# Row maxima of a 64 MB array: loads issued alternately from the SP and the Activation queue

## The chip, the cores and the metric

One core of one Trainium2 chip. The metric is the device time of one execution in microseconds (us); the median of several executions is quoted. More than one chip took part, so each kernel is compared with the runs of the kernel before made in the same series.

## The reference

```python
def setup_inputs():
    batch, seq, dim = 32, 512, 1024
    return {"x": np.random.randn(batch, seq, dim).astype(np.float32)}

def reference(x):
    return np.max(x, axis=-1).astype(np.float32)
```

That is 16,384 rows of 1,024 floats: 64 MB are read, 64 KB written.

## The kernel before

Each of the 128 partitions owns 128 consecutive rows. 112 of them come as 28 "bulk" tiles of four rows (2 MB each), the last 16 as 8 "tail" tiles of two rows (1 MB). Every tile is loaded by one DMA and reduced by one instruction on the vector engine (DVE) into a column block of `res`. There are two stores, one after the bulk and one at the end.

```python
    GB = 4
    GT = 2
    TAIL_ROWS = 16
    NB = (I - TAIL_ROWS) // GB      # 28
    NT = TAIL_ROWS // GT            # 8
    SPLIT = I - TAIL_ROWS           # 112

    bulk = ctx.enter_context(tc.tile_pool(name="bulk", bufs=10))
    tailp = ctx.enter_context(tc.tile_pool(name="tailp", bufs=5))
    # ... (res, out_r, xr)
    for c in range(NB):
        b = c * GB
        xc = bulk.tile([P, GB, D], mybir.dt.float32)
        nc.sync.dma_start(out=xc, in_=xr[:, b:b + GB, :])
        nc.vector.reduce_max(out=res[:, b:b + GB], in_=xc, axis=mybir.AxisListType.X)

    nc.scalar.dma_start(out=out_r[:, :SPLIT], in_=res[:, :SPLIT])

    for t in range(NT):
        b = SPLIT + t * GT
        xt = tailp.tile([P, GT, D], mybir.dt.float32)
        nc.sync.dma_start(out=xt, in_=xr[:, b:b + GT, :])
        nc.vector.reduce_max(out=res[:, b:b + GT], in_=xt, axis=mybir.AxisListType.X)

    nc.scalar.dma_start(out=out_r[:, SPLIT:], in_=res[:, SPLIT:])
```

The framework under it adds the semaphores; two things of it show in the traces. It keeps at most eight DMAs in flight, counted over both queues, and it may move a store past a load on its queue.

## Time and profile before

| | before |
|---|---|
| time, median of 4 runs | 166.98 us (166.93 to 167.51) |
| span of the profiled execution | 166.5 us |
| DMA engines | full, some 428 GB/s from 4 to 158 us |
| DVE | 85% busy; 4.42 us a bulk tile, which lands every 4.89 us |
| last bulk reduce starts / last reduce ends | 141.82 / 164.09 us |

How to read the lines in the prediction: in the slices each digit is the busy tenths of one fortieth of the span. A group has its source line, engine, operation, output and input, then the count, busy time and mean duration in ns, and after the second bar the idle time just before, with what ended it. In a timeline the first two numbers are start and duration in us, `x7` is seven instructions merged into one row, and the bracket holds the idle time before and its cause. `SPq` and `ACTq` are issues on the two queues. A ring is the list of transfers that one queue has pending on one DMA engine; a packet is one record of such an engine, here one row of a tile (16 KB in the bulk, 8 KB in the tail).

### The profile page before, as it was taken

To read this page: it belongs to the slowest core of one execution; us is meant where nothing else is said; L and a number is where in the kernel's file an instruction comes from. 1 tells how busy PE (TensorE), PEld (TensorE's weight loads), DVE (VectorE), ACT (ScalarE), POOL (GpSimd) and SP (SyncE) were. 2 spreads that over 40 slices of the span, in tenths; PEclk is the share of its full clock that TensorE was granted. 3 is DMA by queue.
4 is the path that set the end of the run, shared out by engine and by line. 5 is a ranking of instruction groups with operands and counts; after the bars stand their busy time and mean duration, and the time that the engine had idled before them with its cause. 6 is when DMAs were issued, how large, how long until landed. Compare 5 with 4: busy or idle time off the path is not lost.

```text
span 166.5 us, 142 instructions
## 1 busy us (share of the span) xinstructions
DVE 141.4 (85%) x36; POOL 0.2 (0%) x4
## 2 busy tenths in 40 slices
DVE  0098887898888798888898888899888889999994
POOL 0000000000000000000000000000000000000000
DMA  5999999999999999999999999999999999999950
GB/s 189 429 441 429 429 394 425 433 437 429 433 421 354 425 433 429 429 429 429 433 421 429 429 429 437 417 429 433 429 433 421 425 433 411 425 417 423 421 222 2
DMA packets 5472, 67.18 MB, mean 404 GB/s; under 512 B 864, under 2 KB 864, under 8 KB 864
## 3 DMA queue, kind: packets, MB, share of 16 engines
q1 hardware_dynamic: 5184, 67.11, 95.7%
q10 hardware_dynamic: 288, 0.07, 0.2%
HBM read 67.11 MB, written 0.07 MB: 403 GB/s over the span
## 4 chain that ended last, share of the span: by engine, by line
DMA 89%; DVE 8%; SPq 1%; issue 0%
DMA xc<-in_x_dram 84%; DMA xt<-in_x_dram 5%; DVE res L59 5%; DVE res L47 3%; SPq L46 1%
## 5 line engine op out<-in xcount | busy, mean ns | idle before, releaser
L47 DVE TENSOR_REDUCE res<-xc 128x4 f32<-128x4096 f32 x28 | 123.8, 4420 | 22.5 <-DMA xc<-in_x_dram 22.5
L59 DVE TENSOR_REDUCE res<-xt 128x2 f32<-128x2048 f32 x8 | 17.8, 2280 | 0.2 <-DMA xt<-in_x_dram 0.2
L80 POOL MEMSET const-bfloat16-1.0<- 128x1 bf16 x1 | 0.1, 103 | 0.0
L80 POOL MEMSET const-uint8-127<- 128x1 uint8 x1 | 0.1, 103 | 0.0
L80 POOL MEMSET const-float32-1.0<- 128x1 f32 x1 | 0.1, 100 | 0.0
L80 POOL MEMSET const-float32-0.0<- 128x1 f32 x1 | 0.1, 99 | 0.2 <-issue 0.2
## 6 DMA issues: line engine op xcount, KB each, us to landing
xc<-in_x_dram SPq DMA_DIRECT2D x28, 2048.0 KB, 39.1
xt<-in_x_dram SPq DMA_DIRECT2D x8, 1024.0 KB, 23.5
out_dram<-res ACTq DMA_DIRECT2D x1, 56.0 KB, 6.8
out_dram<-res ACTq DMA_DIRECT2D x1, 8.0 KB, 1.4
```

What stands on the lines that cost most here:

```text
L46: nc.sync.dma_start(out=xc, in_=xr[:, b:b + GB, :])
L47: nc.vector.reduce_max(out=res[:, b:b + GB], in_=xc, axis=mybir.AxisListType.X,)
L59: nc.vector.reduce_max(out=res[:, b:b + GT], in_=xt, axis=mybir.AxisListType.X,)
L80: nc = _bacc.Bacc("TRN2", target_bir_lowering=False, num_devices=1)
```

## The change

Loads go in turn to the SP queue (`nc.sync`) and the Activation (ACT) queue (`nc.scalar`), with the intent that no single queue's issuing holds up the transfers.

```diff
     for c in range(NB):
         b = c * GB
         xc = bulk.tile([P, GB, D], mybir.dt.float32)
-        nc.sync.dma_start(out=xc, in_=xr[:, b:b + GB, :])
+        (nc.sync, nc.scalar)[c % 2].dma_start(out=xc, in_=xr[:, b:b + GB, :])
 ...
     for t in range(NT):
         b = SPLIT + t * GT
         xt = tailp.tile([P, GT, D], mybir.dt.float32)
-        nc.sync.dma_start(out=xt, in_=xr[:, b:b + GT, :])
+        (nc.sync, nc.scalar)[t % 2].dma_start(out=xt, in_=xr[:, b:b + GT, :])
```

## The prediction

> **What bounds the kernel now.** I read the page of the kernel before from the top, and first the slices of the span with the DMA totals.
>
> ```profile
> span 166.5 us, 142 instructions
> DVE 141.4 (85%) x36; POOL 0.2 (0%) x4
> DVE  0098887898888798888898888899888889999994
> DMA  5999999999999999999999999999999999999950
> GB/s 189 429 441 429 429 394 425 433 437 429 433 421 354 425 433 429 429 429 429 433 421 429 429 429 437 417 429 433 429 433 421 425 433 411 425 417 423 421 222 2
> ```
>
> The 16 DMA engines are full from the second slice to the thirty-eighth, at about 428 GB/s. VectorE (DVE) is nearly as busy, 85%, which matters below. Next the groups and the waits: which engine waits for which.
>
> ```profile
> L47 DVE TENSOR_REDUCE res<-xc 128x4 f32<-128x4096 f32 x28 | 123.8, 4420 | 22.5 <-DMA xc<-in_x_dram 22.5
> L59 DVE TENSOR_REDUCE res<-xt 128x2 f32<-128x2048 f32 x8 | 17.8, 2280 | 0.2 <-DMA xt<-in_x_dram 0.2
> ...
> SPq L46 <- DMA xc<-in_x_dram: 90.5, 20, 5.4
> ```
>
> The first line: every bulk reduce waits for its load, 8.24 us for the first and 0.47 for most others. The last line, from the waits of the SP queue: the queue stands waiting 90.5 us, and 20 of the 28 bulk issues wait for a load to land. 28 less 20 is 8: eight loads are in flight, and the ninth is issued at 8.23 us, when the first lands. So issuing is not short of anything: the queue is eight loads (39 us from issue to landing) ahead. Last the timeline of the end.
>
> ```profile
> 136.92 4.42 DVE L47 TENSOR_REDUCE res<-xc 128x4 f32<-128x4096 f32 x1 [0.47 <-DMA xc<-in_x_dram]
> 141.82 4.42 DVE L47 TENSOR_REDUCE res<-xc 128x4 f32<-128x4096 f32 x1 [0.48 <-DMA xc<-in_x_dram]
> 146.16 15.47 DVE L59 TENSOR_REDUCE res<-xt 128x2 f32<-128x2048 f32 x7
> 146.27 0.38 ACTq L53 DMA_DIRECT2D out_dram<-res  x1
> 148.47 4.71 SPq L58 DMA_DIRECT2D xt<-in_x_dram  x3
> 161.80 2.29 DVE L59 TENSOR_REDUCE res<-xt 128x2 f32<-128x2048 f32 x1 [0.17 <-DMA xt<-in_x_dram]
> 164.12 0.34 ACTq L65 DMA_DIRECT2D out_dram<-res  x1
> ```
>
> Loads land every 4.89 us (136.92 to 141.82), a reduce takes 4.42. From 141.82 on, DVE runs without a gap: the last bulk reduce and seven tail reduces (2.19 us from start to start) fill the 19.8 us in which the tail's 8 MB arrives, and the last tail reduce waits just 0.17 us for its load. Both limits meet there: DMA has priority by 0.17 us. Any bulk tile that comes later than today at the end makes DVE the bound.
>
> **What the Trainium skill says.** "DMA: Bandwidth & Descriptors", section "Issuing engines are not separate DMA queues": DMAs from SP, ACT and GpSimd run on the same 16 engines, and a second issuer saves only sequencer time. The trace agrees in what it can show: the engines are full with one issuer, and the sequencer's time, 0.33 us an issue against 4.89 us of transfer, is hidden.
>
> The same page, section "Queues, rings and completion order": SP and ACT own one ring each on every engine, and an engine takes turns between rings that have work, packet by packet. The packet records of before show it at one place: the 56 KB store from the ACT queue has 8 rows on each engine, and while tail loads run, these rows come one every 0.327 us, that is one 8 KB load packet (0.31) and one store row (0.025) in turn. The store takes so 6.8 us to land, against 1.4 for the 8 KB store of equally many rows at the end.
>
> "Perfetto Trace Analysis", section "DMA Instruction — HWDGE (DVE, Sync)": the descriptor generator is locked by one instruction at a time. Before can't show two issuers at the start; if so, ACT's first load gets its descriptors some 0.37 us (the first issue's duration) after SP's.
>
> **The change part by part.** It removes no instruction and no byte. 14 bulk and 4 tail issues move to the ACT queue.
>
> 1. Issue time: 18 × 0.33 = 6 us leave SP. All lay beside transfers. Gain: 0; at the very start at most 0.3 us, as engines draw their first packet at 1.74 us and the second queue can't move that.
> 2. Bytes: 64 MB at 428 GB/s is 157 us, as now. A bulk row of 16 KB takes 0.611 us on its engine and 8 of them 4.89, exactly the spacing of landings: there is no bubble between loads that a second ring could fill. Gain: 0.
> 3. Order of landing: this is the cost. Today load c has all engines to itself. With two rings in turn, loads c and c+1 share them, each takes 9.78 us, and if both rings start together they land together. DVE starts at about 13.0 instead of 8.24, which costs nothing itself (it has 0.47 us spare per load). What counts is the end. Call L the number of 16 KB packets by which SP's ring leads ACT's on each engine; strict turns keep L as it is. The last bulk data lands at about T = 141.8 as today, plus L × 0.31 (the 8 KB tail packets that SP's ring has then already moved); load 26, on SP's ring, lands at T − L × 0.611. From the start of load 26's reduce with both loads there, DVE needs 2 × 4.34 (start to start, 141.82 to 146.16) + 7 × 2.19 + 2.29 = 26.3 us without a gap; today it needs 22.27 from 141.82 to 164.09.
>    - L = 0: load 26 at 141.8, DVE ends at 168.1: +4.0 us.
>    - L = 1 (SP merely first in each turn): 141.2, end 167.5: +3.4.
>    - L = 4 (rings half a load apart): loads land evenly again, load 26 at 139.4, 27 at 143.0; reduce 27 starts at 143.7, DVE ends at 165.7: +1.6.
>    - L = 8 (SP a whole load ahead): loads 25 and 26 land together at 136.9, 27 at 144.3; reduce 27 starts after two others, at 145.6; end 167.6: +3.5.
> 4. The tail's own waits: tail loads 5 to 7 need buffers of tails 0 to 2 and are issued some 3 us later than today (148.47, 150.66, 152.85). They then land at about 157 to 162, and DVE, late itself, wants the last at 163 to 166. Hidden.
> 5. What follows the last reduce (2.4 us to the span's end) stays, and the time is 0.5 above the span, as before.
>
> **Where L falls.** Both queues leave the starting barrier at the same time. The generator's lock puts ACT about 0.4 us behind, which alone is L = 1. But the store on ACT shows that an engine has more already taken in: its first row moved 3.5 us after its issue began, against 1.0 for the first load of the run, so some 2.5 us of SP's packets stood ahead. If that happens at the start, L is about 4. I give L of 0 or 1 about 0.35, 2 to 6 about 0.45, 7 or 8 about 0.2: mean +2.8 us.
>
> **The rivals.**
> - Nothing happens or a small gain: two rings hide a bubble or the slow spots (slices with 394 and 354 GB/s). Against it: packets follow each other at 0.611 us and the slow spots are packets of 1.2 to 2.4 us on half of the engines, not missing descriptors. It would give 165.5 to 167.
> - The store as a block: the first store now stands in ACT's in-order queue with four tail loads and waits for the last bulk reduce. If tail loads 1 and 3 stand behind it, they are issued only at about 150, land at 155 or later, and DVE waits some 3 us more: 173 to 174. Against it: in before, the tail issues are at 107.55, 112.44 and 122.24, and none at the landing of 117.3, so the store took that place in the order of semaphores; it is moved past tail loads rather than kept where the code has it. I give it 0.06.
> - Two streams of rows disturb each other in HBM and the rate falls: 1% is 1.6 us more, 171 to 172. The trace speaks neither for nor against it, as SP's loads had no second load beside them.
> - Paired landing with L from 0 to 8, as worked out: 168.6 to 171.0.
>
> **Range and chances.** 166.98 + 2.8 = 169.8; a little weight on the first rival takes it to 169.7. Low 168.0 (even staggering, faster start), high 171.8 (pairs and 0.5% less rate). The 2% line is 170.3, or +3.34 us: reached with L of 0, 1 or 8, a blocked tail or a lower rate. That makes slower 0.33, within 2% 0.64, faster 0.03.
>
> **What would show it.** The DMA slices should read about 428 GB/s as before, the loads' time to landing stay near 39 us, and the first reduce start between 10.5 and 13 us instead of 8.24. Right: DVE's waits of bulk reduces come in pairs, one long and one near zero (or even, if L is near 4), and DVE runs from load 26 to the end without a gap, with load 26's landing and the DVE end matching one line of the list. Wrong, if a bulk load lands 4.89 us after its predecessor from 8.24 on (no taking turns), if the last tail reduce still waits for its load, if the slices show another rate, or if a tail reduce waits for a load on ACT that was issued after the first store.

## The result

The changed kernel took 171.2 us (median of 4 runs, 171.16 to 171.23) against 166.98: ratio 1.0243, 95% interval 1.0228 to 1.0258, so it is slower by 2.4%. (A ratio here and below is the mean time of one kernel's fast runs over that of the other's of the same rounds, so not quite the ratio of the medians.) The page of the changed kernel, for slices, totals and groups:

```profile
span 169.4 us, 142 instructions
DVE 140.0 (83%) x36; POOL 0.2 (0%) x4
DVE  0008979798997979799797979979797997999994
DMA  5999999999999999999999999999999999999900
GB/s 174 433 422 433 433 433 433 426 433 433 433 422 433 426 418 426 430 426 433 426 433 433 433 430 426 433 422 418 430 422 433 433 420 418 422 383 344 373 29 2
...
L47 DVE TENSOR_REDUCE res<-xc 128x4 f32<-128x4096 f32 x28 | 122.4, 4414 | 27.0 <-DMA xc<-in_x_dram 27.0
L59 DVE TENSOR_REDUCE res<-xt 128x2 f32<-128x2048 f32 x8 | 17.6, 2276 | 0.0
...
xc<-in_x_dram ACTq DMA_DIRECT2D x14, 2048.0 KB, 39.1
xc<-in_x_dram SPq DMA_DIRECT2D x14, 2048.0 KB, 39.1
```

The DMA engines run at the old rate for the old length and a load still lands 39.1 us after its issue. What is new is at both ends. DVE starts a slice later. At the end DVE is full (9) in both kernels, but the transfers now fall behind it: 383, 344, 373 and 29 GB/s in slices 36 to 39, against 417, 423, 421 and 222 before. The tail reduces wait for nothing, 0.0, where the last one before waited 0.17 us for its load. The timeline of the changed kernel, its beginning and its end:

```profile
0.73 0.39 ACTq L46 DMA_DIRECT2D xc<-in_x_dram  x1
0.73 0.37 SPq L46 DMA_DIRECT2D xc<-in_x_dram  x1
...
13.38 8.74 DVE L47 TENSOR_REDUCE res<-xc 128x4 f32<-128x4096 f32 x2 [13.38 <-DMA xc<-in_x_dram]
23.17 8.74 DVE L47 TENSOR_REDUCE res<-xc 128x4 f32<-128x4096 f32 x2 [1.04 <-DMA xc<-in_x_dram]
...
140.69 8.74 DVE L47 TENSOR_REDUCE res<-xc 128x4 f32<-128x4096 f32 x2 [1.06 <-DMA xc<-in_x_dram]
149.35 17.63 DVE L59 TENSOR_REDUCE res<-xt 128x2 f32<-128x2048 f32 x8
149.47 0.35 ACTq L53 DMA_DIRECT2D out_dram<-res  x1
151.66 4.72 ACTq L58 DMA_DIRECT2D xt<-in_x_dram  x2
167.01 0.35 ACTq L65 DMA_DIRECT2D out_dram<-res  x1
```

Reduces now come in twos: 9.79 us from pair to pair, one wait of 1.04 us for two tiles. The semaphore records show why: loads 0 and 1 landed at 13.36 and 13.53, loads 26 and 27 at 140.66 and 140.84. So at 140.69 DVE has two bulk tiles in hand, where before it had one at 141.82, and from there it works without a gap: 8.66 for two bulk tiles, 17.63 for the tail, ending at 166.98. Before, it ended at 164.09.

### The profile page after: what moved, and what is told of

It reads as the page before. It is cut to its first block, busy times and chain, and to the rows that moved or that the text cites. A ratio compares the mean times of both kernels' runs of the same rounds, so it can differ in the third digit from the quotient of the medians.

```text
span 169.4 us, 142 instructions
## 1 busy us (share of the span) xinstructions
DVE 140.0 (83%) x36; POOL 0.2 (0%) x4
## 4 chain that ended last, share of the span: by engine, by line
DMA 82%; DVE 14%; DVEq 1%; SPq 0%; issue 0%
DMA xc<-in_x_dram 82%; DVE res L59 9%; DVE res L47 5%; DVEq L91 1%; SPq L46 0%
## 5 line engine op out<-in xcount | busy, mean ns | idle before, releaser
L47 DVE TENSOR_REDUCE res<-xc 128x4 f32<-128x4096 f32 x28 | 122.4, 4414 | 27.0 <-DMA xc<-in_x_dram 27.0
## 6 DMA issues: line engine op xcount, KB each, us to landing
xc<-in_x_dram ACTq DMA_DIRECT2D x14, 2048.0 KB, 39.1
xc<-in_x_dram SPq DMA_DIRECT2D x14, 2048.0 KB, 39.1
```

## The experiments

My theory: an engine takes the two rings in turn, so partner loads land together, and DVE, which has no slack at the end, gets its last bulk tiles in a lump. Rivals: the ACT queue is a slower issuer; two rings lower the transfer rate; the tail loads are held behind the store in the ACT queue; or the cost lies outside the span, since the two profiles differ by 2.9 us and the times by 4.2. Twelve kernels ran, in three series of four.

**1. The kernel before again.** No edit.

> The unchanged kernel as its own control. Every theory expects a ratio of 1.000 within 0.3%, 167.0 us. It is also a second look at two points of the first profile: the two slow spots of the loads (at 23 and 51 us, together some 1.2 us) and the gap between span and time, which was 0.5 us there and is 1.8 us for the changed kernel. If the slow spots belong to that one execution, this profile shows the last bulk load landing at about 140.4 instead of 141.8 and a span of about 165.2, 1.8 us below the time; if they belong to the kernel, the span is 166.5 again and the missing 1.3 us of the changed kernel lie outside its span.

Measured 167.66 us, ratio 0.9978 (0.994 to 1.0017). Its four executions and the seven beside it all have a time 1.73 to 1.86 us above their span, as have the four of the changed kernel. So none of the loss lies outside the span. The spans of the four quoted executions of before are not on record. If the same 1.8 us holds for them, the profile with 166.5 us belongs to an execution of about 168.3 us, longer than the four; a typical one has a span of 166.98 - 1.8 = 165.2, and the change cost 4.2 us in spans as in times. What can make executions of before differ is in the packet records: at 23 us, and again at 51, eight of the sixteen DMA engines had a packet of 1.2 to 2.4 us instead of 0.611. Here they were at 23, 38 and 75 us. The expectation left two cases open, and it was a mix: the slow spots come each time, at changing places and sizes.

**2. The mirror: all loads on ACT, the stores on SP.**

```diff
-        nc.sync.dma_start(out=xc, in_=xr[:, b:b + GB, :])
+        nc.scalar.dma_start(out=xc, in_=xr[:, b:b + GB, :])
-    nc.scalar.dma_start(out=out_r[:, :SPLIT], in_=res[:, :SPLIT])
+    nc.sync.dma_start(out=out_r[:, :SPLIT], in_=res[:, :SPLIT])
```
(and likewise for the tail and the last store)

> All loads from the Activation queue, both stores from SP: still one ring for the loads. Theory (partners of two rings land together and the vector engine has no slack at the end): nothing lands together, so 167.0 us, ratio 1.000 within 0.5%. Rival (loads issued from Activation are themselves slower or start later): at least half of the change's loss, 169 us or more.

Measured 167.64 us, ratio 0.9983 (0.9947 to 1.0019). The ACT queue is as good an issuer as SP; that rival falls.

**3. Two queues, one tile.** Each tile's halves on the two queues:

```diff
-        nc.sync.dma_start(out=xc, in_=xr[:, b:b + GB, :])
+        H = GB // 2
+        nc.sync.dma_start(out=xc[:, :H, :], in_=xr[:, b:b + H, :])
+        nc.scalar.dma_start(out=xc[:, H:, :], in_=xr[:, b + H:b + GB, :])
```
(the tail likewise, a row each)

> Both queues, but the two halves of one tile: rows 0 and 1 of each bulk tile from SP, rows 2 and 3 from Activation, and one row each in the tail. Packets take turns as in the changed kernel, but partners now serve the same reduce. Theory: tiles are complete every 4.89 us as before, first reduce at about 8.5, 167.0 us within 0.7. Rival (two rings in turn lower the rate of the DMA engines, or cost something outside the span): 170 us or more, with the slices below 428 GB/s or the gap of time over span larger than in the control.

Measured 170.61 us, ratio 1.0156 (1.0116 to 1.0196): my number was missed and the rival's was met. The timeline of the split kernel:

```profile
8.62 4.42 DVE L49 TENSOR_REDUCE res<-xc 128x4 f32<-128x4096 f32 x1 [8.62 <-DMA xc<-in_x_dram]
13.59 4.42 DVE L49 TENSOR_REDUCE res<-xc 128x4 f32<-128x4096 f32 x1 [0.55 <-DMA xc<-in_x_dram]
```

Tiles are indeed complete one by one again, from 8.62 us, but every 4.97 us. Halving the tile had changed a second thing, the length of a row: 8 KB packets took 0.311 us, not half of 0.611. Experiment 5 takes this apart.

**4. Stagger: hold back the first ACT load.** (against the changed kernel)

```diff
         xc = bulk.tile([P, GB, D], mybir.dt.float32)
+        if c == 1:
+            nc.gpsimd.memset(xc[:, 0, :1024], 0.0)
         (nc.sync, nc.scalar)[c % 2].dma_start(out=xc, in_=xr[:, b:b + GB, :])
```

> The changed kernel, with the first Activation load held back by a memset of 1024 columns of its tile on GpSimd, some 1 to 3 us. Theory: SP's ring then leads by L packets of 16 KB, L being the hold in us over 0.611, and keeps that lead to the end; partners land apart by the 0.2 us of the changed kernel plus twice the hold (both measured late in the run, up to 4.9 us), load 26 lands earlier by one hold, and the time falls below 171.2 by about the hold, for a hold of 2.4 us to 168.7. Rival (the loss is in the DMA rate, in the issue or outside the span): time unchanged at 171.2 or longer by the hold, as loads start later.

Measured 169.03 us, ratio 1.0055 (1.0017 to 1.0094) against 1.0243 of the change. The timeline of the staggered kernel:

```profile
0.73 0.95 POOL L47 MEMSET xc<- 128x1024 f32 x1 [0.29 <-POOLq L82]
...
1.71 103.38 ACTq L48 DMA_DIRECT2D xc<-in_x_dram  x14
...
134.07 13.07 DVE L49 TENSOR_REDUCE res<-xc 128x4 f32<-128x4096 f32 x3 [1.04 <-DMA xc<-in_x_dram]
147.06 17.63 DVE L61 TENSOR_REDUCE res<-xt 128x2 f32<-128x2048 f32 x8
```

Starting loads later made the kernel faster by 2.3 us (span 167.1 against 169.4, last reduce ending at 164.69 against 166.98). A loss of rate, or of time to issue, would not shrink when loads start later. The hold was 0.98 us (the 1 to 3 us expected were a guess that no run stood behind), and a gain of about the hold was expected; the lead was more: SP's loads landed at 10.72, 20.50, 30.29 and ACT's at 16.59, 26.37, that is 5.87 and 3.91 us apart in turn. ACT's first packet moved at 5.50, SP's at 1.73. A hold of 1 us let 2 us more of SP's packets go ahead. The lead of 5.87/2 = 2.9 us is 4.8 packets by the landings, and it was kept through the bulk (loads 24 and 25 at 128.19 and 134.05). Loads 26 and 27, at 137.98 and 142.05, are closer, as SP's ring had by then gone over to the shorter rows of the tail.

**5. The control of experiment 3: both halves from SP.**

```diff
-        nc.scalar.dma_start(out=xc[:, H:, :], in_=xr[:, b + H:b + GB, :])
+        nc.sync.dma_start(out=xc[:, H:, :], in_=xr[:, b + H:b + GB, :])
```
(against experiment 3; the tail likewise)

> The control for the split tile: the same two halves of each tile, but both from SP. The split kernel came out at a ratio of 1.0156 and its tiles were complete every 4.97 us instead of 4.89. If that comes from the smaller packets (8 KB rows took 0.311 us, 16 of them 4.98), this kernel has the same 4.97 with one queue and a ratio of 1.011 to 1.022. If it comes from two rings taking turns, tiles come every 4.89 us here and the ratio is within 0.5% of 1.

Measured 169.69 us, ratio 1.0085 (1.0027 to 1.0142), a little under the range. The timeline:

```profile
8.40 4.42 DVE L49 TENSOR_REDUCE res<-xc 128x4 f32<-128x4096 f32 x1 [8.40 <-DMA xc<-in_x_dram]
13.37 4.42 DVE L49 TENSOR_REDUCE res<-xc 128x4 f32<-128x4096 f32 x1 [0.55 <-DMA xc<-in_x_dram]
```

With one queue tiles come every 4.97 us too. The small rows, not the second ring, cost 27 × 0.08 = 2.2 us of the bulk. Experiments 3 and 5 differ by 0.9 us in the medians of two series; that rest is not settled. Experiment 3's profile has 1.3 us of waits in its tail, this one 0.6.

**6. Only the bulk alternates.**

```diff
-        (nc.sync, nc.scalar)[t % 2].dma_start(out=xt, in_=xr[:, b:b + GT, :])
+        nc.sync.dma_start(out=xt, in_=xr[:, b:b + GT, :])
```
(against the changed kernel)

> Only the bulk loads alternate, the tail is all on SP. Theory: the vector engine is late by the last bulk pair and runs without a gap from there, so the tail's queue doesn't matter: ratio 1.021 to 1.027 as for the whole change. Rival (the loss comes from tail loads behind the store in the Activation queue, or from tail loads landing in pairs): less than half of the loss, ratio below 1.012.

Measured 171.47 us, ratio 1.0183 (1.0128 to 1.0239): below the range, and by the ratio alone unclear, as its interval takes in the 2% line; this series' runs of before were scattered (167.31 to 169.49). But the time is that of the whole change (171.2, in another series) and the span, 169.5, too. The end of its timeline:

```profile
140.81 8.75 DVE L47 TENSOR_REDUCE res<-xc 128x4 f32<-128x4096 f32 x2 [1.03 <-DMA xc<-in_x_dram]
149.47 17.62 DVE L59 TENSOR_REDUCE res<-xt 128x2 f32<-128x2048 f32 x8
149.59 0.35 ACTq L53 DMA_DIRECT2D out_dram<-res  x1
```

No tail load is on ACT, so the store can hold none back, and the loss is there in full. That rival falls.

**7. Only the tail alternates.**

```diff
-        (nc.sync, nc.scalar)[c % 2].dma_start(out=xc, in_=xr[:, b:b + GB, :])
+        nc.sync.dma_start(out=xc, in_=xr[:, b:b + GB, :])
```
(against the changed kernel)

> Only the eight tail loads alternate. Theory: bulk loads land evenly as before; only tail partners share engines, and if the last two land together the last reduce starts 2.2 us after the last landing, so +1 to +2 us, ratio 1.006 to 1.012, with waits of the tail reduces for their loads. Rival as in the run before this: most of the loss is here, ratio above 1.015. It has one ring in the bulk, so if the slow spots (half of the engines with packets of 1 to 2 us, seen in each one-queue profile and in no two-queue one) belong to one ring, they are here again, and not in the run with the bulk alternating.

Measured 172.31 us, ratio 1.024 (1.0172 to 1.0308): about twice the +1 to +2 us that I expected, and by the ratio as much as the whole change (1.0243), though this interval takes in the 2% line too. Bulk loads do not come in pairs here, and the store did not do it: the tail reduces wait for nothing. Its timeline:

```profile
111.84 12.60 ACTq L58 DMA_DIRECT2D xt<-in_x_dram  x2
...
117.35 4.42 DVE L47 TENSOR_REDUCE res<-xc 128x4 f32<-128x4096 f32 x1 [1.09 <-DMA xc<-in_x_dram]
124.10 4.42 DVE L47 TENSOR_REDUCE res<-xc 128x4 f32<-128x4096 f32 x1 [2.34 <-DMA xc<-in_x_dram]
129.62 4.42 DVE L47 TENSOR_REDUCE res<-xc 128x4 f32<-128x4096 f32 x1 [1.10 <-DMA xc<-in_x_dram]
136.38 4.42 DVE L47 TENSOR_REDUCE res<-xc 128x4 f32<-128x4096 f32 x1 [2.34 <-DMA xc<-in_x_dram]
```

Two tail loads were issued on ACT at 111.84 and 124.1, into a ring with nothing in it. They took every other turn from the bulk loads queued on SP and landed at 123.17 and 135.40, before bulk loads 23 (124.08) and 25 (136.35), though DVE needed them only after load 27. The bulk was late by their bytes: load 27 landed at 146.15, against 141.37 in experiment 1, and DVE ended at 168.13 against 163.66. It is the theory's principle in a form that I had not foreseen: two rings give up the order of arrival. In the full change ACT's tail loads stand behind ACT's own bulk loads and can't overtake.

**8. A longer tail.** The changed kernel with `TAIL_ROWS = 32`.

> The changed kernel with the last 32 instead of 16 rows as two-row tiles. Theory: the last four-row pair lands at 121.1 and 121.3 (as measured), so the vector engine starts its run without a gap there and needs 2 x 4.34 + 15 x 2.19 + 2.29 us: 164.9, and with the last pair landing together at about 161.1 not before 165.6, against 167.0 in the changed kernel: ratio about 1.013 (1.008 to 1.018). Rival (the loss doesn't depend on the slack of the vector engine): ratio 1.024 or, with more and smaller transfers, above.

Measured 170.58 us, ratio 1.013 (1.0073 to 1.0188). The end of its timeline:

```profile
121.28 8.75 DVE L47 TENSOR_REDUCE res<-xc 128x4 f32<-128x4096 f32 x2 [1.06 <-DMA xc<-in_x_dram]
129.94 26.64 DVE L59 TENSOR_REDUCE res<-xt 128x2 f32<-128x2048 f32 x12
...
156.78 2.29 DVE L59 TENSOR_REDUCE res<-xt 128x2 f32<-128x2048 f32 x1 [0.20 <-DMA xt<-in_x_dram]
```

Given more small tiles DVE caught up: from 156.78 on it waits for loads again. About half of the loss is gone, as expected.

**9 and 10. Half the work for DVE** (results wrong, each reduce reading 512 of its 1,024 columns), on the kernel before and on the changed one.

```diff
-            in_=xc,
+            in_=xc[:, :, :D // 2],
```
(and `xt` likewise)

> Wrong result on purpose: the kernel before, each reduce reading only the first 512 of its 1024 columns, so the vector engine's work is about halved (2.3 us for a bulk tile as for 2048 elements in the tail, 1.2 in the tail) and the loads are unchanged. The last reduce waits for the last load: 1.1 us less than the kernel before, ratio 0.990 to 0.997.

> Wrong result on purpose: the changed kernel with halved reduces, pair to the run before this. Theory (the loss is the vector engine's missing slack behind partners that land together): only the last tail pair still costs, one reduce of 1.1 us, less what the one-ring loads lose in their slow spots: ratio to the kernel before 0.990 to 1.001, at most 1 us above its half-work partner, where the change itself cost 4 us. Rival (the loss is in the transfers, the issue or the store): 3 us or more above its partner, ratio 1.012 or more.

Measured 166.67 us (ratio 0.9928, 0.9879 to 0.9977) and 166.53 us (0.9912, 0.9869 to 0.9954), beside 167.84 of the kernel before: both within what was expected. With slack on DVE the alternation costs nothing. The last lines of the two timelines, half-work before and then half-work changed:

```profile
158.84 1.22 DVE L59 TENSOR_REDUCE res<-xt 128x2 f32<-128x1024 f32 x1 [1.27 <-DMA xt<-in_x_dram]
161.30 1.22 DVE L59 TENSOR_REDUCE res<-xt 128x2 f32<-128x1024 f32 x1 [1.24 <-DMA xt<-in_x_dram]
```

```profile
150.77 2.34 DVE L59 TENSOR_REDUCE res<-xt 128x2 f32<-128x1024 f32 x2 [2.63 <-DMA xt<-in_x_dram]
153.42 1.22 DVE L59 TENSOR_REDUCE res<-xt 128x2 f32<-128x1024 f32 x1 [0.30 <-DMA xt<-in_x_dram]
158.52 3.50 DVE L59 TENSOR_REDUCE res<-xt 128x2 f32<-128x1024 f32 x3 [3.88 <-DMA xt<-in_x_dram]
```

Tiles still land in lumps in the second (three reduces in a row at 158.52), and DVE now swallows them.

**11. Alternate in the first 16 bulk loads only.**

```diff
-        nc.sync.dma_start(out=xc, in_=xr[:, b:b + GB, :])
+        (nc.scalar if c % 2 and c < 16 else nc.sync).dma_start(out=xc, in_=xr[:, b:b + GB, :])
```

> The change in the first 16 bulk loads only (8 from Activation, 8 from SP); the other 12 bulk loads and the tail all from SP. Theory: the pair of loads 14 and 15 leaves the vector engine 4 us late; with loads again every 4.89 us and reduces every 4.34 it makes up 0.55 a load and is level by about load 23, so nothing is left at the end: ratio 0.993 to 1.003, and the last tail reduce waits for its load or starts with it. Rival (alternating costs in proportion to the loads it touches): 16 of 36, ratio about 1.010.

Measured 167.48 us (6 runs), ratio 0.9965 (0.9931 to 0.9999). The end of its timeline:

```profile
140.94 4.42 DVE L47 TENSOR_REDUCE res<-xc 128x4 f32<-128x4096 f32 x1 [0.47 <-DMA xc<-in_x_dram]
145.28 15.48 DVE L59 TENSOR_REDUCE res<-xt 128x2 f32<-128x2048 f32 x7
160.92 2.29 DVE L59 TENSOR_REDUCE res<-xt 128x2 f32<-128x2048 f32 x1 [0.17 <-DMA xt<-in_x_dram]
```

Sixteen alternating loads cost nothing at the end: DVE was level again from load 23 (its reduce at 121.37 waited for its load), and the last lines are those of the kernel before.

**12. A try at a faster version:** experiment 11 with `TAIL_ROWS = 24`, and the last two-row tile loaded and reduced row by row.

```diff
-        nc.sync.dma_start(out=xt, in_=xr[:, b:b + GT, :])
-        nc.vector.reduce_max(out=res[:, b:b + GT], in_=xt, axis=mybir.AxisListType.X)
+        step = GT if t < NT - 1 else 1
+        for r in range(0, GT, step):
+            nc.sync.dma_start(out=xt[:, r:r + step, :], in_=xr[:, b + r:b + r + step, :])
+            nc.vector.reduce_max(out=res[:, b + r:b + r + step], in_=xt[:, r:r + step, :],
+                                 axis=mybir.AxisListType.X)
```

> A try at a version faster than both: as the run before this, with 24 rows in two-row tiles at the end instead of 16, and the last of them loaded and reduced as two single rows. The longer tail lets the vector engine be level with the loads before the end (it gains 0.3 us per two-row tile), and then the last reduce is of one row, 1.15 us instead of 2.29; some 0.2 us are lost to smaller rows. Ratio 0.989 to 0.997. If the vector engine isn't level by then, 0.998 to 1.003.

Measured 167.58 us, ratio 0.997 (0.9936 to 1.0004): no better than experiment 11, and not clear of the kernel before. The end of its timeline:

```profile
156.34 2.29 DVE L63 TENSOR_REDUCE res<-xt 128x2 f32<-128x2048 f32 x1 [0.20 <-DMA xt<-in_x_dram]
158.83 4.54 DVE L63 TENSOR_REDUCE res<-xt 128x2 f32<-128x2048 f32 x3 [0.21 <-DMA xt<-in_x_dram]
```

DVE was level, but the two single rows had to queue behind the two-row tile ahead of them: 4.54 us of work from a landing at 158.81, while the last row landed at 161.32. I had counted just the last reduce. To gain, the rows before it must be small as well. No version here clearly beats the kernel before.

## Why the prediction was right or wrong

The time, 171.2, lay in the range, and the mechanism was the one described. The centre (169.7) and the likeliest class (within 2%) were off. The 0.33 for "slower" was also less than the prediction's own list gives: L of 0, 1 and 8 all pass the line of +3.34 us, and L of 0 or 1 alone had 0.35. These are the steps:

- **What bounds the kernel, steps 1 and 2** (issue time and bytes are worth nothing): right. The mirror changes nothing, and two rings carry the old rate: 430 GB/s from 13.4 to 101 us, against 426 in experiment 1.
- **Step 3, order of landing:** right in the mechanism. The line for L = 0 asks 26.3 us from load 26's reduce to the end; measured 166.98 - 140.69 = 26.29. But the line for L = 1 was wrong. It lets a load land with its eighth row, so that SP, merely first in each turn, would land 0.61 + 0.31 us ahead and cost +3.4. SP was first in each turn: on each DMA engine ACT's first packet came after one of SP's. Yet all partners landed 0.17 to 0.18 us apart. The packet records show why. After the rows of a load comes one more packet of 4 bytes on each engine, which reports the landing, and it takes a turn of its own: all 208 of SP's between 10 and 138 us began as a row of ACT's ended, and ACT's own followed 6 ns later. (The records don't name the engine; the packets are matched by their times.) So SP's lead of one row was lost, and L = 1 cost what the list gives for L = 0.
- **"Where L falls" is the other step that failed.** I took the 2.5 us that the store had waited behind SP's packets as possible at the start too, and spread L over 0 to 8 with a mean of +2.8. That wait was seen only beside a ring that already had work: from issue to first packet 3.5 us for the store, 3.8 for the held load in the stagger experiment, 3.4 for the tail load at 111.84 in experiment 7. When both queues started together ACT's first packet came 1.1 us after SP's, just as SP's own first packet (1.08 us) ended. The generator's lock doesn't show either: both first issues run from 0.73 us, for 0.39 and 0.37 us.
- **The base:** the span of 166.5 was paired with a time of 166.98, giving 0.5 us between them; it is 1.73 to 1.86 in every execution whose span is on record. So the profiled execution must have been a slow one. In the list L = 0 gave +4.0 us, and the times differ by 4.2; the profiles only by 2.9, since the changed kernel's last bulk load landed at 140.84, 1 us before that of the slow execution.
- **The start:** "at most 0.3 us" of gain was a loss: the first pair was complete at 13.53, where load 1 of before landed at 13.09.
- **Step 4** and the rival of the blocking store: two tail loads did stand behind the store (issued from 151.66, when the first tail reduce had just freed a buffer) and no reduce waited for them.
- **The rival of the hidden slow spots**, put aside, had something in it: with rows of 16 KB, eight engines lost 1.1 to 2.2 us each on average to slow packets between 5.5 and 130 us in the five profiles with all bulk loads on one ring, and at most 0.2 in the five with the bulk alternating to the end. But experiments 11 and 12 had them (at 17 us and later) while both rings were at work, and experiment 5, on one ring with 8 KB rows, lost 0.3; so rings alone don't explain them. The cause is open.

## What to carry to other kernels

When the transfers are full, ask of a second queue not what it adds but what it reorders: two rings share the engines packet by packet, so loads finish in lumps, and a load put into an empty ring overtakes those queued before it. That is harmless while the consumer has slack to the end of the kernel (half-work reduces: no loss; alternation stopped 12 loads before the tail: no loss) and costs about one reduce where it has none (4.2 us here, a bulk reduce being 4.42). Before pairing a profile with a time, check that they belong to the same execution.

## What the Trainium skill lacked or had wrong

- "DMA: Bandwidth & Descriptors", "Issuing engines are not separate DMA queues": it is right that the engines are shared and no bandwidth is gained, but the only effect that it names is the issue time saved. Here the second issuer cost 2.4%, as a pair of loads lands every 9.79 us instead of one every 4.89; and with only the tail alternating, loads on the empty ring overtook older ones and delayed the last bulk load by 4.8 us.
- The same page, "Queues, rings and completion order": the turns by packet agree with the runs, but where the page gives a packet some 9 to 17 descriptors, the rings here changed after every row (16 KB, 0.611 us). It doesn't tell that the packet which reports a landing takes a turn of its own (208 of 208 of SP's came after a row of ACT's, so partners landed 0.17 to 0.18 us apart through the whole bulk), nor that a ring which starts beside a working one moves late: 0.98 us of hold put ACT's first packet 3.8 us behind SP's, where without the hold it was 1.1.
- "Perfetto Trace Analysis", "DMA Instruction — HWDGE (DVE, Sync)": the exclusive lock on the generator, with the wait for it inside the reported time, isn't seen at the start: the first issues on SP and ACT run together from 0.73 us and take 0.37 and 0.39, and SP's first issue alone took 0.37. Only the fourth issues are longer, 0.96 and 1.02 against 0.66 with one issuer; why is open.
- No page that I read has the slow spots: eight of sixteen engines with one packet of 0.7 to 2.4 us instead of 0.611, up to three times in a run; executions of the kernel before ranged from 166.93 to 169.49 us over four series, those of the changed kernel, in one series only, from 171.16 to 171.23.
